# Two-layer hybrid trunk: more projection steps early in the chunk recurrence, and one turn ahead of its Newton step

## The chip, the cores and the metric

One core of a Trainium2 chip. The metric is the device time of one execution in microseconds; the kernel before takes 2350.74 us (median of three runs, 2348.04 to 2352.05). TensorE is called PE here, VectorE DVE, ScalarE ACT, GpSimd POOL, and SyncE, which issues the transfers, SP.

## The reference

Two layers run over 640 tokens of 1024 channels: 128 context tokens and 512 latent ones. Each layer normalises and modulates its input to `h`, projects it (`z = h @ w_in`), and feeds four mixers: a bidirectional recurrent mixer (8 heads with a 64 x 64 state), latent attention, gated position mixing, and a Fourier mixer. Their gated outputs are merged and projected back onto the residual.

The change lies in the recurrent mixer. For each direction it computes, token after token,

```
sa = S @ (-kk)
S  = S * w + outer(sa, kk * a) + outer(v, k)
y  = S @ r
```

for the context (starting from zero) and for the latents (starting from a given state); the outputs of both directions are added.

## The kernel before

All tokens stay on the chip; a tile holds 128 channels in its partitions and the 640 tokens in its columns. A projection chunk of 128 output channels is computed in two halves of 320 tokens. For each of the eight tiles of `h` there are three matmuls (high and low parts of weights and activations), so a half is 24 matmuls; `dense_half` (L161) yields after every two tiles, that is after six matmuls. A chunk is therefore eight such steps, and `fill` (L462), which makes the chunks that later mixers need, adds a ninth when it has stored one to DRAM (`zdr`, L470). Weights come by SP, are rounded by ACT (L144) and the rest is taken by POOL (`wl`, L145).

The recurrence (`recurrence`, L676) goes through 64-token chunks: 2 of the context and 8 of the latents, for two directions, 20 jobs. `intra` (L700) is the part of a job that needs no state. Its steps: loads (L708, L710); decays and keys (L722 to L749); products within the chunk (L757) and their mask; the matrix in two float16 parts; the transposed keys (L776); then the inverse of a 64 x 64 triangular matrix for each head by doubling. The first level starts at L787 to L790; five levels follow, each of two steps: L807 on PE and L808 on DVE, then L814/L815 on PE and the sum L818 on DVE. A Newton step closes it: L823/L824 on PE with L826 on DVE, then L830/L833 with the copy L835 and two copies L838 on ACT. `chain` (L841) is the part with the state, four steps (L847, L854, L860, L868/L870), in the order of the chunks.

A turn of the main loop (L885) advances each chain and each active job by one step; the chains come first, then the oldest job. A job starts every 6 turns (`STAG`), at most 4 are active (`NACT`). With its 21 steps a job in one turn at its last level stands beside one at level 2, one at its matrix parts and one at its loads. `mix` (L97) emits steps of the `fill` chunks after each turn: 1.2 + 0.1 * (5 - running) of them, so 1.6 while one job runs and 1.3 with four (L1230). What is left is emitted after the last turn.

The kernel is written in a framework that records what is emitted and then orders the instructions of each engine ahead of the run, by the order of emission and its own estimate of when operands and buffers are ready. Each engine then runs its list in that order; a late operand holds all that stands behind it. Chunks of `fill` use three PSUM banks (`d`), the recurrence five (`m`). Behind the recurrence comes the first merge (`merge`, L1126): it loads the branch output (`load_o`, L1113: `f<-odr`, ACT, then DVE or POOL), and its first product (`w_merge`, 48 matmuls) needs only `h`.

Of the kernel before, what the change touches and what calls it, by code (L numbers as in the profile page):

```python
# [14 lines left out]
DRAM = bass.MemoryType.DRAM  # L15
# [3 lines left out]
T = 640  # L19
# [6 lines left out]
RATE_R = 1.2  # L26
RATE_R1 = 0.1
RATE_M = (0.25, 0.5, 0.55, 0.5)
NACT = 4
# [27 lines left out]
def trunk(ctx: ExitStack, tc: tile.TileContext, A: dict, O: dict, dbg: dict):  # L57
# [39 lines left out]
    def mix(main, side, rate):  # L97
        """Emit the steps of main, with rate steps of side after each."""
        owed = 0.0
        for n in main:  # L100
            owed += rate(n) if callable(rate) else rate
            while owed >= 1.0:
                next(side, None)
                owed -= 1.0

    def settle(side):
        """Go on to the end of a projection chunk."""
        while next(side, CHUNK_END) != CHUNK_END:
            pass

# [41 lines left out]
    def wload(src, n, leng=None):  # L152
        """Weights in their high and low parts"""
        hi = wp.tile([128, 512], F32R, tag="wh", name="wh", bufs=3)
        lo = wp.tile([128, 512], F32R, tag="wl", name="wl", bufs=3)
        split(hi[:, :n], lo[:, :n], raw_load(src, n), leng)
        return hi, lo
# [3 lines left out]
    def dense_half(w, K, act, use, q, step=2):  # L161
        """use(tokens, psum) with psum[f, tok] = w^T act for the tokens q, three float32r passes."""
# [21 lines left out]
    def rsqrt(out, x, n=T):  # L184
        """out = x ** -0.5: table value, then one Newton step."""
# [6 lines left out]
    def colsum(lhs, rhs, use):  # L192
        """use(cols, psum) for the two halves of lhs^T rhs"""
        for q in HALVES:
            ps = bank1()[:, :320]
            mm(ps, lhs, rhs[:, q], start=True, stop=True)
            use(q, ps)
# [35 lines left out]
    def ada(l, ns, bufs):  # L233
        """Modulation chunks: the tiles of the contraction in four column groups, summed with the turn to feature-major."""
# [30 lines left out]
    def sum_squares(acc, x, k, q, last=None):  # L265
        """acc[:, q] += x^2; the last of the chunks stays apart, for the sum on the tensor engine."""
# [24 lines left out]
    def norm_tile(l, h, xr, k, q):  # L291
        """h[k] at the tokens q from the normalised x, in its high and low parts"""
# [12 lines left out]
    def norm_first(h, X, q):  # L305
        """The first norm, up to its modulation"""
# [19 lines left out]
    def norm_half(l, h, X, q):  # L326
        """RMSNorm and modulation of one half of the tokens"""
# [8 lines left out]
    # ================= one layer =================  # L336
    def layer(l, X, h, w13):
# [17 lines left out]
        def shift(c, z, out):  # L355
            """out = z + (centred_shift(z) - z) * mu for the chunk c of the projection."""
# [7 lines left out]
        def silu2(c, out):  # L364
            """2 * silu of the chunk c of the projection"""
# [17 lines left out]
        def low_rank(kp, src, w):  # L383
            """tanh(0.5 * (bias + up^T src)) for both directions, in the order of their scans, to DRAM."""
# [30 lines left out]
        def unit(xa, c):  # L415
            """the keys' unit vectors"""
# [7 lines left out]
        def proj_rkv(kp, z13):  # L424
            def turn(c, v):
                """the values, token-major"""
# [15 lines left out]
            for nth, c in enumerate((4, 5, 6, 7, 0, 1, 2, 3, 8, 9, 10, 11)):  # L442
                z = kp.tile([128, T], F32, tag="k", name="rkv")
                # within each half and after the chunk: a step of the low-rank products
# [29 lines left out]
        def attention(z13, xa, side):  # L474
            with tc.tile_pool(name=f"at{l}", bufs=1) as ap_, tc.tile_pool(name=f"a2{l}", bufs=2) as a2:
# [16 lines left out]
                # normalised compressed kv and q  # L492
# [32 lines left out]
                # values, token-major  # L525
                def values(vhalf):
                    vv = a2.tile([128, 6, 4, 128], F32R, tag="vv", name="vv", bufs=1)
                    wv_hi, wv_lo = aload(A["w_v"][l, :, 256 * vhalf:256 * vhalf + 256], 256)
                    for tt in range(6):
# [5 lines left out]
                        # high and low parts side by side; the high part in the rows where the head's output goes  # L535
# [64 lines left out]
                def weighted(pn, vv, pr, j, kt, o):  # L600
                    """add the key block kt (0: context rows, 1-5: latent rows) to the outputs of one head"""
# [74 lines left out]
        def recurrence(y):  # L676
            with tc.tile_pool(name=f"rw{l}", bufs=1) as rw:
# [9 lines left out]
                # block-diagonal operands of a pair of heads; what lies outside the blocks stays zero  # L687
# [12 lines left out]
                def intra(seg, i, d, A16, XZ):  # L700
                    """The state-independent part of one 64-token chunk in one direction (8 heads)."""
# [33 lines left out]
                    # modified keys  # L735
# [4 lines left out]
                    # rows of the products: A keys then K keys for even heads, the other way for odd ones;  # L740
                    # the K keys meet the values and stay in the order of the tokens in both directions
# [9 lines left out]
                    # intra-chunk products, masked  # L751
# [11 lines left out]
                    # A^T - I  # L763
# [3 lines left out]
                    # in two parts of float16  # L767
# [15 lines left out]
                    # X = (I - A)^-1 and its transpose by doubling in float16, then one Newton step  # L783
# [8 lines left out]
                    for lev in range(1, 6):  # L792
                        if lev == 2:
                            # token-major values
# [4 lines left out]
                        # the even blocks of columns of X and the odd ones of its transpose change  # L799
# [19 lines left out]
                        yield  # L819
                    ps = bank1()  # L820
# [15 lines left out]
                    # the rows of A make room for the queries of the carried state  # L836
# [47 lines left out]
                nact, since, count = NACT, 99, 0  # L884
                while order or active or chains or jobs:  # L885
# [6 lines left out]
                    # the sequential parts first  # L892
                    if order and len(chains) < 2 and order[0] in done and not any(c[0][0] == order[0][0] and c[0][2] == order[0][2] for c in chains):
# [8 lines left out]
                        chains.append((jb, chain(done.pop(jb), d, state[s_, d])))  # L902
                    running = len(chains) + len(active)
# [13 lines left out]
                    yield running  # L917

# [52 lines left out]
        # ---- Fourier mixing: channels first (only the half that the symmetry leaves), then positions with the odd / even symmetry;  # L971
        # channel k of two groups comes as e - d, channel 128 - k as e + d ----
        def fourier():
            with tc.tile_pool(name=f"fd{l}", bufs=1) as c1, tc.tile_pool(name=f"fe{l}", bufs=2) as c2:
# [10 lines left out]
                # cosine and sine parts of the four groups; the cosine parts of channel 64, each in a column of its own  # L985
# [31 lines left out]
                def pos(stat, tts, o, n):  # L1017
                    """over the positions: the product of the stationary operand's tiles with the table at o"""
# [43 lines left out]
        def rec_out(y):  # L1062
            with tc.tile_pool(name=f"gn{l}", bufs=2) as gp:
# [6 lines left out]
                def sums(x, use):  # L1070
                    """use(cols, psum) with the sums over the channels of each head, in two float32r passes"""
# [12 lines left out]
                for c in range(4):  # L1084
# [4 lines left out]
                    # sum of both directions' modified keys, then the bonus  # L1089
# [56 lines left out]
        # ================= emission =================  # L1146
        fl = fill()
        with ExitStack() as es:
# [3 lines left out]
            # the first four chunks wait for the norm, half by half  # L1152
            with tc.tile_pool(name=f"first{l}", bufs=1, side="right") as fp:
# [14 lines left out]
                if l == 0:  # L1168
                    # in the order in which the inputs come: the products over the first four tiles of h
                    # run before the modulation of the others is there  # L1170
# [57 lines left out]
        with tc.tile_pool(name=f"y{l}", bufs=1, side="right") as yp:  # L1228
            y = yp.tile([128, 4, T], F32, name="y")
            mix(recurrence(y), fl, lambda n: RATE_R + RATE_R1 * (5 - n))  # L1230
# [23 lines left out]
    def in_weights(l):  # L1254
        """the weights of the first chunk that a layer computes"""
        return [wload(A["w_in"][l, 13][:, k * 128:k * 128 + 512], 512) for k in (0, 4)]

    def output(l, mh, ml, w0):
        """x + gate * (merged w_out), half of the tokens after the other; what follows starts on the first half."""
# [73 lines left out]
    # ================= program =================  # L1333
# [20 lines left out]
def _layout(i):  # L1354
# [6 lines left out]
    def ktile(w, m):  # L1361
        """[K, M] -> [128, K/128 * m-chunk]: one m-wide column chunk, k-tiles side by side."""
# [12 lines left out]
    # the order in which the Fourier mixing leaves its channels  # L1375
# [52 lines left out]
    # constants of the shapes alone  # L1428
# [79 lines left out]
```

## Time and profile before

| | us |
|---|---|
| runs: median (lowest, highest) | 2350.74 (2348.04, 2352.05) |
| span of the profiled execution, first to last instruction | 2346.5 |
| PE busy / DVE busy / ACT busy / POOL busy | 2204.5 / 1459.3 / 1099.2 / 890.0 |
| recurrence of layer 0 | about 384 to 729 |
| recurrence of layer 1 | about 1543 to 1886 |

The profiled execution has no time of its own in the page beside its span; the median of the runs is 4.2 us above that span. Busy time is the time in which an engine works on at least one instruction; matmuls overlap, so it isn't the sum of their durations. A wait is put down to the instruction that waited and the one that came last before it. PEclk is the clock granted to PE: 1.00 is 2.4 GHz, and a window that mixes it with 1.2 GHz has a value between 0.5 and 1. `fill` appears as tile `f`, matmuls of L168 to L170 as `dps`.

### The profile page before, as it was taken

What the parts mean: (1) busy time and instruction counts of PE and PEld (TensorE: products, weight loads), DVE (VectorE), ACT (ScalarE), POOL (GpSimd) and SP (SyncE); (2) the same over time, 40 slices, a digit from 0 to 9 for tenths busy, and PEclk for the clock granted to TensorE, in tenths of its full rate; (3) what the DMA queues carried; (4) which work ended last, traced back from release to release, by engine and by line L of the source; (5) the groups of instructions that cost most, each with busy time, mean ns of one, the idle gap of its engine ahead of it and who ended that gap; (6) DMA issues with size and microseconds to landing.
All of it is one profiled execution on the core that took longest, in us unless ns stands there. A gap on an engine that the chain in (4) does not pass through costs nothing. (4 is left out here: it accounts for less than half of the span.)

```text
span 2346.5 us, 49722 instructions
## 1 busy us (share of the span) xinstructions
PE 2204.5 (94%) x19662; PEld 2017.0 (86%) x19662; DVE 1459.3 (62%) x2826; ACT 1099.2 (47%) x2387; POOL 890.0 (38%) x894
## 2 busy tenths in 40 slices
PE   6899998898999999999998999989999999999998
PEld 3788898787889998978998888978888899989997
DVE  4767756888884435642267777578888643367325
ACT  4566755444444333432355667544444343344332
POOL 2322124444443344533453221254444334355452
PEclk8999999999999999999999999999999999999999
DMA  7133336333225425556432333362322254254332
GB/s 260 50 105 92 92 91 195 95 109 98 79 65 169 139 85 173 143 194 240 131 121 71 97 98 98 97 213 84 104 77 76 72 171 151 75 172 144 105 106 101
DMA packets 208009, 283.73 MB, mean 121 GB/s; under 512 B 26912, under 2 KB 119712, under 8 KB 207776
## 3 DMA queue, kind: packets, MB, share of 16 engines
q1 hardware_dynamic: 207776, 280.55, 38.2%
q8 instruction: 155, 2.54, 0.5%
q14 instruction: 78, 0.64, 0.1%
HBM read 224.75 MB, written 55.74 MB: 120 GB/s over the span
## 5 line engine op out<-in xcount | busy, mean ns | idle before, releaser
L145 POOL TENSOR_TENSOR wl<-wr,wh 128x512 fp32r<-128x512 f32 x371 | 520.7, 1407 | 988.4 <-ACT wh L144 846.0
L168 PE MATMUL dps<-hhi,wh 128*128 128x320 f32 x2368 | 773.4, 327 | 12.9 <-DVE f L1133 4.9
L169 PE MATMUL dps<-hlo,wh 128*128 128x320 f32 x2368 | 744.1, 314 | 7.4 <-POOL hlo L299 4.5
L170 PE MATMUL dps<-hhi,wl 128*128 128x320 f32 x2368 | 742.5, 314 | 0.8 <-POOL wl L145 0.8
L168 PEld LDWEIGHTS dps<-hhi,wh 128*128 128x128 f32 x2368 | 452.2, 191 | 33.2 <-issue 8.2
L169 PEld LDWEIGHTS dps<-hlo,wh 128*128 128x128 f32 x2368 | 452.5, 191 | 15.4 <-POOL hlo L299 6.8
L170 PEld LDWEIGHTS dps<-hhi,wl 128*128 128x128 f32 x2368 | 451.5, 191 | 6.1 <-issue 3.7
L144 ACT CAST wh<-wr 128x512 fp32r<-128x512 f32 x372 | 229.3, 619 | 290.4 <-PE dps L169 175.0
L169 PE MATMUL dps<-olo,wh 128*128 128x320 f32 x512 | 161.5, 316 | 9.5 <-POOL olo L145 5.2
L168 PE MATMUL dps<-ohi,wh 128*128 128x320 f32 x512 | 161.2, 316 | 3.7 <-ACT ohi L144 3.6
L170 PE MATMUL dps<-ohi,wl 128*128 128x320 f32 x512 | 159.3, 311 | 0.0
L818 DVE TENSOR_TENSOR XZ<-XZ,m 128x512 f16<-128x512 f16 x200 | 129.5, 677 | 47.9 <-PE m L815 47.7
L1133 DVE SCALAR_TENSOR_TENSOR f<-f,dps 128x320 f32<-128x320 f32 x96 | 46.4, 485 | 138.8 <-PE dps L170 127.1
L765 POOL TENSOR_TENSOR GG<-GG,con 64x256 f32<-64x256 f32 x80 | 61.2, 765 | 163.6 <-DVE GG L760 160.3
L1131 ACT ACTIVATE f<-dps,der 128x320 f32<-128x320 f32 x128 | 67.2, 525 | 113.9 <-PE dps L170 112.1
L169 PEld LDWEIGHTS dps<-olo,wh 128*128 128x128 f32 x512 | 97.1, 190 | 14.8 <-POOL olo L145 6.8
L168 PEld LDWEIGHTS dps<-ohi,wh 128*128 128x128 f32 x512 | 96.8, 189 | 6.9 <-ACT ohi L144 5.0
L170 PEld LDWEIGHTS dps<-ohi,wl 128*128 128x128 f32 x512 | 97.2, 190 | 0.0
L808 DVE TENSOR_TENSOR T<-m,con 128x256 f16<-128x256 f32 x200 | 80.5, 415 | 18.1 <-PE m L807 17.6
L611 DVE TENSOR_TENSOR pl<-m,ph 128x512 fp32r<-128x512 f32 (+1 forms) x96 | 59.3, 620 | 28.5 <-ACT ph L610 27.3
L770 ACT CAST A<-GG 64x256 f16<-64x256 f32 x80 | 32.3, 404 | 90.9 <-POOL GG L765 90.9
L814 PE MATMUL m<-T,XZ 128*128 128x64 f16 x800 | 66.1, 195 | 5.8 <-DVE T L808 5.8
(492 smaller groups left out, 4645.4 us busy)
## 6 DMA issues: line engine op xcount, KB each, us to landing
wr<-in_w_in SPq DMA_DIRECT2D x180, 256.0 KB, 3.0
wr<-in_w_merge SPq DMA_DIRECT2D x128, 256.0 KB, 2.9
ar<-in_w_ada SPq DMA_DIRECT2D x48, 512.0 KB, 6.6
wr<-in_w_branch SPq DMA_DIRECT2D x64, 256.0 KB, 2.8
zdr<-f SPq DMA_DIRECT2D x48, 320.0 KB, 3.5
rk<-spill SPq DMA_DIRECT2D x20, 768.0 KB, 6.0
thdr<-t SPq DMA_DIRECT2D x32, 320.0 KB, 2.9
odr<-t SPq DMA_DIRECT2D x32, 320.0 KB, 3.4
```

What stands on the lines that cost most here:

```text
L144: S_.copy(hi, src)
L145: (leng or G).tensor_sub(lo, src, hi.bitcast(F32))
L168: mm(ps, hi[:, c], ahi(k)[:, q], start=(k == 0), stop=False)
L169: mm(ps, hi[:, c], alo(k)[:, q], start=False, stop=False)
L170: mm(ps, lo[:, c], ahi(k)[:, q], start=False, stop=(k == K - 1))
L611: V.tensor_sub(pl[:, 0:w], tp[:, 0:w], ph[:, 0:w].bitcast(F32))
L765: G.tensor_sub(GK[HALF[j], j], GK[HALF[j], j], bc(i64[HALF[j]], 4))
L808: V.tensor_mul(T1.rearrange("p u (j k o i) -> p (u j) k o i", j=2, o=2, i=b)[:, :, :, 0, :], ps[:, 0:256].rearrange("p (x k i) -> p x k i" ...
L814: mm(ps[:, 64 * u:64 * u + 64], X1[:, u, :], cols(T1[:, u, :], 0), start=True, stop=True)
L818: V.tensor_add(new, new, ps.rearrange("p (x n i) -> p x n i", x=2, i=b))
L1131: yield from dense(A["w_merge"][l, m, n], 8, H, lambda q, ps: S_.activation(gt[:, q], ps, AF.Tanh, scale=0.5, bias=bias))
L1133: yield from dense(A["w_branch"][l, n, m], 4, o, lambda q, ps: V.scalar_tensor_tensor(to[:, q], gt[:, q], 1.0, ps, op0=ALU.add, op1=ALU.mult))
```

## The change

`intra` gets one more `yield`, after the last doubling level and ahead of the Newton step: a job has 22 steps. The rate of `fill` steps is now yielded by the recurrence itself: 3.5 for each of the first 4 turns, 2.0 for turns 5 to 18, and from there the same 1.2 + 0.1 * (5 - running). Comments and docstrings are removed as well.

```diff
                         V.tensor_add(new, new, ps.rearrange("p (x n i) -> p x n i", x=2, i=b))
                         yield
+                    yield
                     ps = bank1()
                     for u, j in units:
...
-                nact, since, count = NACT, 99, 0
+                nact, since, count, turn = NACT, 99, 0, 0
                 while order or active or chains or jobs:
...
                         chains.append((jb, chain(done.pop(jb), d, state[s_, d])))
+
+                    turn += 1
+                    lead = 3.5 if turn <= 4 else 2.0 if turn <= 18 else None
                     running = len(chains) + len(active)
...
-                    yield running
+                    yield lead or RATE_R + RATE_R1 * (5 - running)
...
-            mix(recurrence(y), fl, lambda n: RATE_R + RATE_R1 * (5 - n))
+            mix(recurrence(y), fl, lambda rate: rate)
             run(fl)
```

## Rows read from the trace of the kernel before

**Rows 1.** The page, busy us (share of the span) and instructions of each engine.

```profile
PE 2204.5 (94%) x19662; PEld 2017.0 (86%) x19662; DVE 1459.3 (62%) x2826; ACT 1099.2 (47%) x2387; POOL 890.0 (38%) x894
```

**Rows 2.** Windows: stretch, length, busy PE PEld DVE ACT POOL, clock, DMA share, GB/s.

```profile
384.00:440.00 56.00, 44.84 (x520) 40.64 (x518) 45.52 (x92) 25.83 (x63) 30.93 (x42) 0.94 0.55 181
440.00:728.00 288.00, 273.04 (x4228) 240.38 (x4226) 230.20 (x491) 123.31 (x307) 120.64 (x158) 0.98 0.27 83
...
1543.00:1600.00 57.00, 45.01 (x527) 40.49 (x526) 46.40 (x94) 26.00 (x64) 32.06 (x45) 0.97 0.57 184
1600.00:1886.00 286.00, 270.89 (x4253) 238.50 (x4251) 230.58 (x491) 123.07 (x307) 120.25 (x158) 0.99 0.27 85
```

**Rows 3.** Line L818, who waited for it: us in total, times.

```profile
  PE m L823: 30.8, 28
  PE m L807: 4.0, 18
```

**Rows 4.** Waits of PE, 440 to 728: us in total, times, longest.

```profile
PE m L823 <- DVE XZ L818: 13.4, 12, 1.8
```

**Rows 5.** Waits of PE in the start-up, layer 0, then layer 1.

```profile
PE m L814 <- DVE T L808: 2.4, 4, 1.0
PE m L823 <- DVE XZ L818: 2.0, 2, 1.3
...
PE m L757 <- DMA thl<-thdr: 4.2, 1, 4.2
```

**Rows 6.** Windows of 5 us with a lower clock.

```profile
395.00:400.00 5.00, 3.83 (x22) 3.64 (x23) 3.02 (x8) 1.88 (x5) 3.21 (x4) 0.56 0.60 189
400.00:405.00 5.00, 4.60 (x26) 4.32 (x26) 5.00 (x8) 4.25 (x12) 4.65 (x9) 0.75 0.69 243
455.00:460.00 5.00, 3.69 (x44) 3.31 (x44) 2.49 (x5) 1.95 (x5) 0.51 (x2) 0.71 0.27 79
...
1745.00:1750.00 5.00, 5.00 (x64) 4.38 (x63) 1.72 (x4) 2.74 (x8) 0.57 (x1) 0.77 0.13 47
```

**Rows 7.** Timeline of a turn change: start, us, engine, line, operation, [idle before <- releaser].

```profile
566.36 0.69 PE L870 MATMUL m<-GG,ZZ 128*64 128x64 f32 x16
...
566.98 0.20 PE L814 MATMUL m<-T,XZ 128*128 128x64 f16 x1
...
567.76 1.28 POOL L145 TENSOR_TENSOR wl<-wr,wh 128x512 fp32r<-128x512 f32 x1
567.79 1.40 DVE L843 COPY ZZ<-S 64x256 f32<-64x256 f32 x1
...
569.12 1.27 DVE L818 TENSOR_TENSOR XZ<-XZ,m 128x512 f16<-128x512 f16 x2
...
569.84 0.22 PE L823 MATMUL m<-XZ,A 64*64 64x64 f16 x2 [1.26 <-DVE XZ L818]
```

**Rows 8.** Timeline: two products of a projection, with L169 and L170 between.

```profile
374.83 0.31 PE L168 MATMUL dps<-hhi,wh 128*128 128x320 f32 x1
...
375.27 0.31 PE L168 MATMUL dps<-hhi,wh 128*128 128x320 f32 x1
```

**Rows 9.** Timeline around the first job's products.

```profile
386.01 0.42 ACT L348 COPY f<-dps 128x320 f32<-128x320 f32 x1
...
396.17 1.22 PE L757 MATMUL m<-Qs,Ks 64*128 64x128 f32 x6 [4.45 <-issue]
```

**Rows 10.** Stores of kept projections, layer 0: first and last of 20.

```profile
386.46 0.32 SPq L470 DMA_DIRECT2D zdr<-f  x1
...
726.18 1.65 SPq L470 DMA_DIRECT2D zdr<-f  x1
```

**Rows 11.** Windows over the end of the recurrence, layer 0.

```profile
704.00:729.00 25.00, 25.00 (x383) 21.74 (x383) 10.11 (x22) 6.04 (x14) 5.11 (x4) 1.00 0.27 81
729.00:738.20 9.20, 8.65 (x66) 7.99 (x62) 1.29 (x3) 6.23 (x9) 4.53 (x3) 1.00 0.80 262
```

**Rows 12.** Line L790: ns min/median/max, first and last start.

```profile
L790 DVE TENSOR_TENSOR XZ<-A,m1T x40: 412/559/1156, 403.2 to 1846.6; 128x512 f16<-128x512 f16 x40
```

## The prediction

> **What bounds the kernel now.** I read the page's busy row first: TensorE (PE) is busy 94% of the span, VectorE (DVE) 62% [rows 1]. So time can only come from the 142 us in which PE is idle, or from stretches in which it is busy at the lower clock. The windows over the two recurrences, the only stage the change touches, say where that is [rows 2]: in layer 0 PE is idle 11.2 us of the first 56 and 15.0 us of the next 288; in layer 1 12.0 us of 57 and 15.1 us of 286. Together 53 us.
>
> The waits by line name the causes. After the start-up, 13.4 of the 15.0 us in layer 0 is one wait: L823, the first product of the Newton step, for the sum of the last doubling level, L818 [rows 4]; over both layers 30.8 us in 28 waits [rows 3]. In the start-up the largest single wait is L757 of the first job, 4.5 us in layer 0 [rows 9] and 4.2 in layer 1, where the load of its decays is named; L823 has only 2.0 us there, the rest is several waits of about 1 us, such as L814 for L808 [rows 5].
>
> The timeline of one turn change shows how the L823 wait arises [rows 7]. PE issues 16 products L814/L815 from 566.98, the last ending at 567.6, and then one step of a kept projection; by 568.6 it has nothing left in its order. DVE meanwhile is in the copy L843, which takes 1.40 us beside a POOL subtraction of 1.28 us, and starts the two sums L818 only at 569.12. L823 starts at 569.84, after 1.26 us of waiting. The turns on either side carry more PE work, which is why L818 is late only here.
>
> Last, the clock. Six separate stretches behind these waits (four in layer 0, two in layer 1) show a granted clock down to between 0.66 and 0.77 in a window of 5 us, where the rest shows 1.00; the first and the last are in [rows 6]. Each loses about 1.7 us, the first 0.29*5 = 1.45 in its own window and the rest in the next; the six 10.2 us. Behind the 4.5 us idle at the start of layer 0 the windows show 0.56 and 0.75: 3.4 us.
>
> **The extra turn.** One `yield` delays L823 by a turn; no instruction is added. The 139 turns of layer 0 take 384 to 729, 2.5 us each, and the longest wait is 1.8, so L818 will be ready and the L823 wait should go: **-30.8 us**. What is late next? Before, L823 stood in front of the next younger job's L807, which needs the other half of the same pair of sums; that L807 waited only 4.0 us in all [rows 3] because L823 had waited for it. Now the chain's last step, moved by the same turn, stands there instead, two groups of 16 matmuls of 0.69 us [rows 7]. So that L807 comes 0.88 (one step) + 1.4 = 2.3 us behind L814/L815, where the pair of sums ended (569.12 + 1.27 = 570.39) 2.8 us behind it: up to 0.5 us of wait, nothing where the turn has two steps. Two turns later the youngest doubling job loses about 0.3 us of PE cover, since the chain's 0.69 us group is replaced by the shorter second Newton product. I take 0.2 us for each of 40 jobs, **+8 us**; the ends are 0 and 23 (three quarters of the wait return).
>
> With the waits shorter than those that low-clock stretches followed, I take **-8 us** of the 10.2 (ends 0 and -10.2). A job lives 22 turns instead of 21 and starts every 6, so still four are alive, and A16, XZ (three copies) have a job's first write three turns behind the last read of the job three before. The turn itself costs nothing while other jobs fill PE; at the end of each recurrence it is one turn without any work of its own.
>
> **More kept projections at the start.** A chunk is nine steps, eight with six matmuls. Their pitch is (375.27 - 374.83)/3 = 0.147 us [rows 8], so a step is 0.88 us and a chunk 7.0 us. Layer 0 stores 20 chunks from 386.46 to 726.18 [rows 10]: 180 steps. Before, turns 1 to 18 emit 6*1.6 + 6*1.5 + 6*1.4 = 27 steps; after, 4*3.5 + 14*2.0 = 42. So 15 steps, 13.3 of them with matmuls, 11.7 us of PE work per layer, go from the end to the start. They bring no work and no transfer that wasn't there.
>
> What they meet: by the time PE reached the first L757, it had run the first chunk and, between that chunk's last evacuation at 386.01 and the idle before 396.17, (391.72 - 386.1)/0.147 = 38 of the second's 48 matmuls [rows 9]: 15 steps, where the turns before had emitted 6. The order of an engine is therefore not that of emission while work is missing; 14 emitted steps don't get past those 15, and I leave the 4.5 and 4.2 us where they are (ends: 0, or all 8.7 and 5 us of clock gained). But behind it the turns 5 to 23 got only some 18 steps (27 + 5*1.3 - 15), and now get 33. There the remaining idle of the start-up, 11.2 - 4.5 - 2.0 = 4.7 us in layer 0 and 12.0 - 4.2 - 2.0 = 5.8 in layer 1, has work to cover it. I take two thirds, **-7 us** (ends 0 and -10.5): DVE is busy 5.00 of 5 us at 400 [rows 6], so some turns will be late whatever PE does.
>
> A row and a rule bear on that. The same DVE instruction L790 takes 0.41 us at least and 1.16 at most [rows 12], and L843 1.40 us beside the POOL subtraction [rows 7]. Each chunk brings two such subtractions, so the 1.67 chunks moved put 3.3*1.28 = 4.3 us of POOL beside a full DVE. The Trainium skill, page "SBUF — State Buffer", section "SBUF: two separate sides", says that the two engines share a port pair that the one that starts first holds for its whole instruction, so that the other is blocked fully. By that, all 4.3 us per layer would be added to DVE and the gain of 7 would be gone, which leaves -22.8 and 2328; the rows show such delays, but not beside every subtraction, so I keep 7.
>
> **The price at the end.** All 180 steps are emitted by turn 136 of 139 before, by 128 of 140 after. PE has no idle at all in 704 to 729 of layer 0 and 0.55 us in the 9.2 us behind it [rows 11]. From turn 128 on 11 steps, 9.7 us, are missing. The first gate product of the merge (48 matmuls, 7.0 us) can move up in their place, as ten of its matmuls already did; but today it covers the loading and splitting of the branch output right behind the recurrence. So per layer the loss lies between 0 (the turns shrink by what left them) and 9.7 + 7.0 = 16.7 us. Without the projections the last 12 turns need some 1.2 us each for product, evacuation and the way back, 14.5 us with 10 us of PE's own work; 7.0 us of merge fit in with about 2.5 too much. I take 4 us per layer, **+8 us**.
>
> **Sum:** -30.8 + 8 - 8 - 7 + 8 = -29.8 us. Span 2346.5 - 29.8 = 2316.7; the median of the runs lies 4.2 us above the span, so **2321 us**, 1.3% less.
>
> **Rivals.**
> *The wait only moves.* DVE's order of prepared work and sums stays, and L807 and L814 wait where L823 did. For it: 4.0 us of L807 waits on the same sum. Against it: mid-recurrence DVE is busy 230 of 288 us. Three quarters return: -30.8 + 23 - 5 (clock) - 4 (start) + 8 = -9: 2342.
> *Slower: the bare end.* Place: turns 128 to 140 and the 8 us behind them. Price 16.7 per layer, 33.4, if those turns are bound by their chain today; and the low-clock stretches aren't saved, only moved behind the new idle, as 4.5 us idle brought one at 395. -30.8 + 8 - 7 + 33.4 = +3.6: 2354. It decides once the end costs more than 15 us per layer.
> *The start is fully covered.* The L757 idle goes too with its low clock (-13.7), the end costs 2 per layer (-4): -48, 2303.
> *The rates do nothing.* If order follows readiness alone, the projections run when they do now: no -7, no +8. -31, 2320; only the store times tell it from the forecast.
>
> **Chances.** Forecast 0.46, with an own range of 2310 to 2334; moved wait 0.17; bare end 0.15; covered start 0.12; rates without effect 0.10. A change under 0.2% (4.7 us) can't be told from none. Faster: 0.44 + 0.10 + 0 + 0.12 + 0.09 = 0.75; within 0.2%: 0.01 + 0.06 + 0 + 0 + 0.01 = 0.08; slower 0.01 + 0.01 + 0.15 = 0.17. The range 2302 to 2350 leaves out the bare end and little else.
>
> **What would show it.** L823's waits for L818 at under 3 us in all, and none of L807 above 12. No window below 0.9 of the clock between 440 and 690. The third and fourth stores of layer 0 behind 386 some 8 us earlier in relation to L757 of job 4, the last store before the last L870. L757's first wait still 4 us. PE idle in the last 25 us of the recurrence and the 9 behind, 3 to 6 us, where it was 0.6. It is wrong if the waits of PE in mid-recurrence add up to over 10 us per layer, or the end to over 10.

## The result: 0.6% slower, and the profile after

The changed kernel takes 2367.6 us (median of four runs, 2363.06 to 2369.59) where the kernel before, timed beside it, takes 2351.39 (2348.04 to 2352.36): a ratio of 1.0062, interval 1.0045 to 1.0078. Forecast were 2321 us and a range of 2302 to 2350; it is slower, and outside the range. The profiled execution took 2369.59 us, its span is 2367.8, so 21.3 us more than the span of before. In the code after, lines behind the added `yield` have numbers higher by one: the Newton step is L824/L825, the chain's steps L848, L855, L861 and L869/L871, the two copies between its second and third step L856 (DVE) and L857 (ACT).

The page's busy row, against [rows 1]:

```profile
PE 2217.0 (94%) x19662; PEld 2022.8 (85%) x19662; DVE 1475.3 (62%) x2826; ACT 1102.1 (47%) x2387; POOL 886.7 (37%) x894
```

Windows like [rows 2] (stretch, length, busy PE PEld DVE ACT POOL, clock, DMA share, GB/s): the two recurrences, then the end of layer 0's recurrence and the first microseconds behind it, as in [rows 11].

```profile
384.00:440.00 56.00, 46.35 (x460) 43.10 (x459) 38.99 (x73) 22.49 (x55) 30.39 (x36) 0.94 0.60 200
440.00:734.00 294.00, 275.69 (x4309) 237.93 (x4308) 243.61 (x507) 126.07 (x313) 119.18 (x163) 0.99 0.25 80
...
1556.00:1613.00 57.00, 48.70 (x473) 45.45 (x472) 39.95 (x77) 23.77 (x57) 30.80 (x39) 0.94 0.65 208
1613.00:1907.00 294.00, 275.67 (x4299) 238.01 (x4297) 243.72 (x507) 126.09 (x313) 119.19 (x163) 0.99 0.26 80
710.00:735.00 25.00, 25.00 (x436) 21.21 (x434) 13.59 (x31) 5.31 (x15) 2.55 (x2) 1.00 0.17 49
735.00:744.20 9.20, 6.50 (x35) 5.33 (x36) 2.43 (x3) 7.80 (x11) 6.16 (x4) 0.89 0.81 251
740.00:750.00 10.00, 8.62 (x39) 7.78 (x39) 3.21 (x6) 6.33 (x12) 2.36 (x3) 0.66 0.99 344
```

In the first 56 us PE idles 9.7 us instead of 11.2, in layer 1 8.3 of 57 instead of 12.0, though the same stretch now holds less of the recurrence (460 matmuls instead of 520, 473 instead of 527). In mid-recurrence PE idles 18.3 us in each layer, where it was 15.0 and 15.1, although the wait that made up nearly all of it has gone. The waits of PE from 440 to 734 (us in total, times, longest), against [rows 4], and who waited for L818 in the whole span, against [rows 3], tell why.

```profile
PE m L861 <- ACT ZZ L857: 10.0, 12, 1.5
PE m L861 <- DVE ZZ L856: 4.0, 6, 1.3
PE m L807 <- DVE XZ L818: 2.8, 3, 2.2
PE m L814 <- DVE T L808: 0.9, 1, 0.9
```

```profile
  PE m L807: 5.6, 6
```

The Newton step waits for nothing any more; 30.8 us are gone. In their place stands L861, the third step of the chain, with 14.0 us in layer 0 and the same 14.0 in layer 1; before, this step had no wait. It waits for the copies of the chain's second step, 20.1 of the 28.0 us for the one on ACT. One such place, in the timeline (start, us, engine, line, operation, [idle before <- releaser]):

```profile
571.98 0.68 PE L855 MATMUL m<-R,Z 64*64 64x64 f32 x16
572.59 0.41 PE L807 MATMUL m<-XZ,A 128*128 128x64 f16 x8
...
573.92 0.33 PE L861 MATMUL m<-ZZ,KT 128*64 128x64 f32 x2
575.75 0.68 PE L861 MATMUL m<-ZZ,KT 128*64 128x64 f32 x14 [1.50 <-ACT ZZ L857]
...
572.52 1.61 POOL L765 TENSOR_TENSOR GG<-GG,con 64x256 f32<-64x256 f32 x2 [1.96 <-DVE GG L760]
...
573.28 0.41 ACT L770 CAST A<-GG 64x256 f16<-64x256 f32 x1 [0.60 <-POOL GG L765]
574.16 0.40 ACT L770 CAST A<-GG 64x256 f16<-64x256 f32 x1 [0.47 <-POOL GG L765]
574.90 0.41 ACT L839 COPY GG<-Qs 64x256 f32<-64x256 f32 x1 [0.34 <-POOL Alo L772]
575.33 0.37 ACT L857 COPY ZZ<-m 64x256 f32<-64x256 f32 x1
```

L855 ends at 572.66, but its ACT copy L857 starts at 575.33: ahead of it in ACT's list stand the two casts L770 of a younger job and a copy L839 of the same job, and all three wait for POOL's subtractions L765 and L772 (0.60, 0.47 and 0.34 us). In the kernel before, this ACT copy started 0.5 to 0.9 us behind the chain's second product; now it is 1.6 to 2.9 us behind it in 17 of layer 0's 20 jobs, and in 16 of the 20 the instruction just ahead of it is L770 or L839. PE meanwhile has 8 small products and one projection step (572.84 to 573.95).

The idle time understates such a wait. The end of a matmul is modelled, so the first part of a wait counts as busy: the first two products of L861 start at 573.92 and the next at 575.75, and of these 1.83 us only 1.50 are called idle. So the stretches are also counted from the start of one matmul to the start of the next, and put down to the later of the two; the text says "from start to start" where it does that.

From the timelines I took the start of the third chain and of the eighteenth; between them lie 15 periods of six turns. "Projection matmuls" are those of L168 to L170. By these marks the stages are (us, layer 0 / layer 1):

| stage | before | after | difference |
|---|---|---|---|
| start, to the third chain (from 384 and 1543.0; after, from the same matmuls at 382.7 and 1556.4) | 77.6 / 76.7 | 88.2 / 89.3 | +10.6 / +12.6 |
| middle, 15 periods | 235.8 / 234.5 | 240.3 / 239.1 | +4.5 / +4.6 |
| from there to the last product of the recurrence | 31.9 / 32.0 | 23.7 / 23.6 | -8.2 / -8.4 |

So the start takes most of what was moved into it (90 and 89 projection matmuls, 13 us at 0.147), the end is shorter by what left it (57 in each layer, 8.4 us), and the middle, where the gain should have been, is longer:

```profile
470.90:711.20 240.30, 225.62 (x3487) 194.72 (x3486) 205.12 (x428) 107.06 (x266) 102.92 (x141) 0.99 0.27 87
```

Against the kernel before (its line stands under the first experiments, with those of e3 and e2) PE is idle 2.0 us more there and busy 2.5 more, with 14 matmuls fewer. From start to start, layer 0's middle has 16.3 us more at L861 (26.8 for 10.5; idle shows 11.3 of it) and 3.9 more at L807, against 12.5 less at the Newton step's first products; projection matmuls, 12 fewer, take 2.4 less and the rest 0.8 less. That is the 4.5 us. In layer 1 it is +16.3, +3.5, -12.8, -2.1 and -0.4. More has come back than went.

The stages make 15.7 us. The other 5.6 of the spans lie outside, nearly all between the recurrences (1120 to 1555 in the profile before): that code, which no edit touches, took 436.0 us before, 441.6 after and 437.7 to 441.8 in the other sixteen traces, so the difference can't be put down to these edits. The medians are 16.2 apart, not 21.3.

### The profile page after: what moved, and what is told of

Its sections match the earlier page's. It is cut to its first block, busy times and chain, and to the rows that moved or that the text cites. A ratio compares the mean times of both kernels' runs of the same rounds, so it can differ in the third digit from the quotient of the medians.

```text
span 2367.8 us, 49714 instructions
## 1 busy us (share of the span) xinstructions
PE 2217.0 (94%) x19662; PEld 2022.8 (85%) x19662; DVE 1475.3 (62%) x2826; ACT 1102.1 (47%) x2387; POOL 886.7 (37%) x894
## 5 line engine op out<-in xcount | busy, mean ns | idle before, releaser
L168 PE MATMUL dps<-hhi,wh 128*128 128x320 f32 x2368 | 771.6, 326 | 17.6 <-ACT f L1135 8.1
L169 PE MATMUL dps<-hlo,wh 128*128 128x320 f32 x2368 | 743.0, 314 | 7.6 <-POOL hlo L299 3.9
L170 PE MATMUL dps<-hhi,wl 128*128 128x320 f32 x2368 | 743.6, 314 | 0.0
L168 PEld LDWEIGHTS dps<-hhi,wh 128*128 128x128 f32 x2368 | 451.0, 190 | 39.2 <-ACT f L1135 9.1
L169 PEld LDWEIGHTS dps<-hlo,wh 128*128 128x128 f32 x2368 | 451.4, 191 | 16.4 <-POOL hlo L299 6.6
L170 PEld LDWEIGHTS dps<-hhi,wl 128*128 128x128 f32 x2368 | 450.7, 190 | 5.0 <-issue 3.7
L169 PE MATMUL dps<-olo,wh 128*128 128x320 f32 x512 | 163.2, 319 | 9.4 <-POOL olo L145 4.8
L168 PE MATMUL dps<-ohi,wh 128*128 128x320 f32 x512 | 163.8, 320 | 3.9 <-ACT ohi L144 3.9
L170 PE MATMUL dps<-ohi,wl 128*128 128x320 f32 x512 | 161.0, 314 | 0.0
L818 DVE TENSOR_TENSOR XZ<-XZ,m 128x512 f16<-128x512 f16 x200 | 132.5, 681 | 39.6 <-PE m L815 39.5
L765 POOL TENSOR_TENSOR GG<-GG,con 64x256 f32<-64x256 f32 x80 | 60.5, 757 | 144.3 <-DVE GG L760 141.3
L169 PEld LDWEIGHTS dps<-olo,wh 128*128 128x128 f32 x512 | 98.7, 193 | 14.5 <-DVE olo L145 6.7
L168 PEld LDWEIGHTS dps<-ohi,wh 128*128 128x128 f32 x512 | 98.4, 192 | 7.2 <-ACT ohi L144 5.4
L170 PEld LDWEIGHTS dps<-ohi,wl 128*128 128x128 f32 x512 | 98.8, 193 | 0.0
L808 DVE TENSOR_TENSOR T<-m,con 128x256 f16<-128x256 f32 x200 | 78.8, 415 | 16.7 <-PE m L807 14.9
L814 PE MATMUL m<-T,XZ 128*128 128x64 f16 x800 | 65.9, 194 | 4.6 <-DVE T L808 4.6
L594 ACT ACTIVATE pe<-sps,st 128x640 f32<-128x640 f32 x64 | 50.8, 794 | 40.3 <-DVE st L592 40.2
```

Of the source, the lines that this page charges most:

```text
L168: mm(ps, hi[:, c], ahi(k)[:, q], start=(k == 0), stop=False)
L169: mm(ps, hi[:, c], alo(k)[:, q], start=False, stop=False)
L170: mm(ps, lo[:, c], ahi(k)[:, q], start=False, stop=(k == K - 1))
L594: S_.activation(pe[:, 0:kn].rearrange("p (b n) -> p b n", n=hn), sv, AF.Exp, bias=st[:, 1:2], scale=scale, accum_out=st[:, 2:3])
L765: G.tensor_sub(GK[HALF[j], j], GK[HALF[j], j], bc(i64[HALF[j]], 4))
L808: V.tensor_mul(T1.rearrange("p u (j k o i) -> p (u j) k o i", j=2, o=2, i=b)[:, :, :, 0, :], ps[:, 0:256].rearrange("p (x k i) -> p x k i" ...
```

## The experiments

Sixteen kernels, each timed in three rounds. The kernel before took 2351.91 us beside e1 to e4 (16 runs), 2351.9 beside e5 to e8 (19), 2351.24 beside e9 to e12 (25) and 2349.93 beside e13 to e16 (8). Ratios are against the runs beside them and have their 95% interval in brackets. Turns are counted from 1. "Cover" is the projection work that PE has between two steps of the recurrence, "the lead" the start's higher rates, and "alignment" which turns the projection steps fall into.

### Each edit alone, and projection steps put where PE waits

**e1**, the extra turn alone (the first hunk of the diff). **e2**, the start's rates alone (the others). **e3**, the kernel before, and **e4**, the extra turn, both with as many projection steps in the middle as before, but more of them in the one turn after which PE waits:

```diff
+                    turn += 1
                     running = len(chains) + len(active)
+                    rate = RATE_R + RATE_R1 * (5 - running)
+                    if 18 < turn <= 121:
+                        rate = 2.0 if turn % 6 == 1 else 1.14   # e4: turn % 6 == 0
...
-                    yield running
+                    yield rate
```

Expected of e1:

> The extra turn alone, the rates of fill steps as before. Theory A (the rates cost, by the end of the recurrence left bare; the turn only moves the wait from L823 to the chain's third step): 2351 us within 5, PE waits of 12 to 16 us per layer at the third chain step (L861), none at the Newton step, and the last store of a kept projection still within 2 us of the last chain's end. Theory B (the turn costs, because the chain now stands in the turns with the least cover and the periods of six turns grow from 15.8 to 16.1 us): 2360 to 2370, with the period of mid-recurrence at 16.1 or more.

Expected of e2:

> The higher rates in turns 1 to 18 alone, a job has 21 steps as before. Theory A (the rates cost): 2362 to 2370; the L823 waits stay at 30 us, the start-up is 7 to 10 us longer per layer, the end only 6 to 9 shorter, and the first merge after layer 0 starts some 5 to 8 us poorer with a window of low clock. Theory B (the turn costs): 2345 to 2353.

Expected of e3:

> The kernel before, with the same number of fill steps in each six turns of mid-recurrence (7.7), but two of them in the turn whose end is the L823 wait and 1.14 in each of the others. Theory C (the wait is a matter of how little PE work stands between the last sum and its reader): the L823 waits of turns 20 to 121 fall from 13 us per layer to under 4, none of the others grows over 4, and the time falls by 12 to 25 us, to 2325 to 2340. Theory D (DVE with its prepared work is the limit, a wait that is taken away returns at another reader): the PE waits in mid-recurrence stay over 10 us per layer and the time within 5 us of 2351.

Expected of e4:

> The extra turn, rates at the start as before, and in mid-recurrence two fill steps in the turn that ends in the chain's third step (L861), 1.14 in each of the others. Theory C: the L861 waits fall from about 14 us per layer to under 4 and the time lies 12 to 25 us under that of the extra turn alone. Theory D: the waits stay over 10 us per layer at other lines and the time within 5 us of the extra turn alone.

| | us | ratio |
|---|---|---|
| e1 extra turn alone | 2363.46 | 1.0046 [1.0033, 1.0060] |
| e2 start's rates alone | 2379.28 | 1.0114 [1.0091, 1.0137] |
| e3 before, cover at the Newton step | 2330.93 | 0.9909 [0.9893, 0.9926] |
| e4 extra turn, cover at the third step | 2349.12 | 0.9987 [0.9977, 0.9996] |

Each edit alone is slower; the extra turn costs 12 us, the rates 27, and together they cost 16, not 39. e3 beats the kernel before by 21 us and leaves every step of a job in its turn. Waits of PE over the recurrence of layer 0 (384 to 735), in the kernel before, e1, e3 and e4:

```profile
PE m L823 <- DVE XZ L818: 15.4, 14, 1.8
```

```profile
PE m L861 <- ACT ZZ L857: 13.3, 16, 1.5
...
PE m L861 <- DVE ZZ L856: 2.4, 3, 1.9
```

```profile
PE m L823 <- DVE XZ L818: 7.6, 8, 1.7
```

```profile
PE m L807 <- DVE XZ L818: 7.4, 10, 2.2
PE m L861 <- ACT ZZ L857: 6.5, 13, 0.9
...
PE m L861 <- DVE ZZ L856: 1.1, 2, 0.9
```

The windows over the 15 middle periods, of the kernel before, e3 and e2:

```profile
461.60:697.40 235.80, 223.16 (x3501) 196.70 (x3500) 198.04 (x424) 106.21 (x266) 105.19 (x141) 0.98 0.28 86
```

```profile
457.00:684.20 227.20, 219.28 (x3499) 193.26 (x3498) 198.22 (x423) 106.22 (x266) 105.20 (x142) 1.00 0.29 90
```

```profile
467.40:715.10 247.70, 229.59 (x3499) 202.39 (x3498) 203.85 (x430) 106.62 (x267) 104.31 (x142) 0.95 0.27 85
```

All three run 3500 matmuls there, within two. Against the kernel before, e3 idles 4.7 us less (7.9 for 12.6) and is busy 3.9 us less with the same matmuls, at a clock of 1.00 instead of 0.98: that is its 8.6 us. e2 idles 5.5 us more and is busy 6.4 more, at a clock of 0.95. One place of e2 shows how the two hang together:

```profile
560.35 0.31 PE L170 MATMUL dps<-hhi,wl 128*128 128x320 f32 x1
562.89 0.22 PE L823 MATMUL m<-XZ,A 64*64 64x64 f16 x2 [2.23 <-DVE XZ L818]
...
564.97 0.47 PE L168 MATMUL dps<-hhi,wh 128*128 128x320 f32 x1
565.24 0.47 PE L169 MATMUL dps<-hlo,wh 128*128 128x320 f32 x1
```

A wait of 2.23 us, and two microseconds behind its end the projection's matmuls go at a pitch of 0.27 us instead of 0.147 [rows 8].

The cover can be counted: in the timelines I counted the projection matmuls that PE runs between the last product of the step before and the one that waits, for each of layer 0's 20 jobs (a step is 6 matmuls).

| wait of | projection matmuls in between | jobs | wait, us |
|---|---|---|---|
| L823, before | 4 to 7 / 12 | 18 / 2 | 15.4 / 0 |
| L823, e3 | 4 to 7 / 12 | 6 / 14 | 6.5 / 1.1 |
| L861, after | 2 to 7 / 12 | 15 / 5 | 12.6 / 1.4 |
| L861, e1 | 2 to 7 / 12 | 15 / 5 | 13.7 / 2.0 |

With about one step a job waits 0.8 to 1.1 us in the mean, with two 0 to 0.4. So theory C stands in its mechanism: the wait hangs on how many steps fall into that turn. Its figure for the waits does not: it had said under 4 us, and 7.6 are left at L823 in e3 and at L861 in e4. By the code, five of e3's six jobs with about one step got a chunk's ninth step, which has no matmul, as one of their two. Theory D (DVE as the limit) falls with e3's time, though in e4 a wait does return at another reader, 7.4 us at L807. Theory A is refuted by e1, theory B by e2, which is 9 us above A's range as well. e4 is 14 us under e1, at the lower end of its 12 to 25.

### Why the extra turn costs: the longer job or the chain's place

```diff
 # e5: the kernel before, the extra turn at the job's start
                     thw, tha = th[:, 0:4, :], th[:, 4:8, :]
                     yield
+                    yield
...
 # e9: the kernel before, an empty turn at the chain's start; e10: e1 with the same
                     Qs, ZZ, GK, GR, Z1, KT, PC, ch, first = it
+                    yield
```

Expected of e5:

> The kernel before, with the one extra turn at the other end of the chunk job: after the job's loads, ahead of its first computation. The job has 22 steps as in the changed kernel, but its later steps keep their places against the chain of carried states and against the neighbouring jobs. Theory P (what costs in the changed kernel is the chain's new place against the neighbouring jobs): the waits behind the ZZ copies at the chain's third step do not come, those at the inverse's Newton step stay near 15 us in a layer, and the time is that of before, 2349 to 2356. Theory N (a job of one more step is dearer wherever the step is, since five runs instead of four stand in more turns and each such turn gets fewer projection steps): 2360 to 2366, as the kernel with the extra turn alone.

Expected of e9:

> The kernel before, with an empty turn at the start of the chain of carried states instead of ahead of the Newton step: the job keeps its 21 steps and its own places, the four steps of the chain stand one turn later against the jobs, as they do in the changed kernel. Theory P (the chain's new place brings the new waits): 8 to 16 us in a layer appear ahead of the chain's third step, behind the ZZ copies; the chain's fourth step now stands ahead of the Newton step in its turn and takes a part of the wait there (15 us before, under 10 now). Both together about even or dearer: 2350 to 2366. Theory N (the longer job costs, not the place): no waits of over 4 us in a layer at the third step and 2346 to 2355.

Expected of e10:

> The kernel with the extra turn alone (e1), and an empty turn at the start of the chain besides: the chain's second and third step then have a turn between them in which two jobs run the second halves of a doubling level (16 matmuls each), not one in which jobs have first halves of 4 each. Theory P: the waits at the third step fall from 16 us in a layer to under 6, those at the Newton step stay away, and the time is 8 to 18 us under e1, 2345 to 2356. Theory N: the job is as long as in e1 and the chain longer, so 2362 to 2370.

e5 took 2358.0 us (1.0021 [1.0011, 1.0031]), e9 2355.89 (1.0024 [1.0014, 1.0033]), e10 2358.88 (1.0031 [1.0016, 1.0045]). Waits of PE over layer 0's recurrence, in e5, e9 and e10 (in e5 the Newton step is L824 and the second half of a level L815; in e10 the chain's second and third steps are L856 and L862):

```profile
PE m L824 <- DVE XZ L819: 12.1, 12, 1.5
PE m L815 <- DVE T L809: 8.9, 13, 1.9
```

```profile
PE m L861 <- ACT ZZ L857: 11.9, 15, 1.5
...
PE m L861 <- DVE ZZ L856: 3.7, 4, 1.9
...
PE m L823 <- DVE XZ L818: 0.8, 1, 0.8
```

```profile
PE m L862 <- ACT ZZ L858: 6.1, 7, 1.4
...
PE m L856 <- ACT R L851: 3.0, 4, 0.9
...
PE m L862 <- DVE ZZ L857: 1.3, 4, 0.4
```

e9 is the cleanest. The job is as long as before and the Newton step where it was; only the chain is a turn later (and the projection steps are dealt to the turns as in e1, since the longer chain counts as running). The waits at the third step come, 15.6 us as in e1 (15.7), and those at L823 go, 15.4 to 0.8, because the chain's fourth step (32 matmuls) now stands just ahead of it, in 19 of layer 0's 20 jobs. So the new place of the chain is what makes the new wait, and it is enough to remove the old one. e5, with the longer job and the chain in its old place, has no wait at the third step and still 12.1 us at the Newton step, nearly what theory P said; but 8.9 us of waits have come ahead of the second half of a level (2.6 before), and its time is 2 us over P's range and 2 under N's. In e10 the third step's waits halve (7.4) but do not fall under 6 as P said; the middle is 8.3 us shorter than e1's, the start 6.0 longer with one more turn for the chain, and 4.6 us of time are left, not 8 to 18: the time is outside both theories' ranges. Against the kernel before, the chain's place alone costs 4.7 us (e9), the longer job alone 6.1 (e5), and the extra turn, which does both, 11.6 (e1).

### Why the start's rates cost 27 us

```diff
 # e6: e3 with the start's rates
+                    if turn <= 18:
+                        rate = 3.5 if turn <= 4 else 2.0
...
 # e7: the kernel before, half a step more in the first turn; e13: half a step less
+                    if turn == 1:
+                        rate += 0.5
 # e14, e15: e2 with half a step less, half a step more; e16: both edits, half a step less
```

Expected of e6:

> The kernel before with the changed kernel's projection rates in turns 1 to 18 and, in turns 19 to 121, the rates of e3 (2.0 in the turn that holds the Newton step's wait, 1.14 in the others). Theory M (the 27 us that the lead rates cost alone are lost in the middle of the recurrence, where the projection steps are as many as before but fall worse, so that idle time grows and the clock drops): a middle made by the phase rule gives most of it back, idle and clock loss there as in e3, and what stays is the start, the bare end and the joins, some 4 to 5 us in a layer: 2337 to 2345. Theory S (the lead costs by itself, through the transfers and buffers that it pulls forward): 2352 to 2360, 27 us over e3.

Expected of e7:

> The kernel before with half a projection step more credited in the first turn alone: every projection step of the recurrence then comes up to one turn earlier or at the same turn, and nothing else is changed. Theory M: the middle's time hangs on which turn a projection step falls into, so even this moves the time by more than 0.2 per cent, by 5 to 15 us to either side. Theory S: nothing of note moves, 2349 to 2355.

Expected of e13:

> The kernel before with half a projection step less credited in the first turn, the counterpart of e7. Theory A (the middle's time hangs on which step falls into which turn, and the kernel before has a good one of several alignments): it moves by 2 to 10 us, more likely up. Theory R (what a half step does is within 3 us, and e7's 4.6 is nearly all there is): 2349 to 2354.

Expected of e14:

> The start's rates alone (e2) with half a projection step less in the first turn. Theory A (a large part of e2's 27 us is its alignment: one step of projection, at times the empty last one of a chunk, ahead of the Newton step): it comes down by 5 to 15 us, 2363 to 2374. Theory R (the lead costs 27 us whatever the alignment): 2376 to 2383.

Expected of e15:

> The start's rates alone (e2) with half a projection step more in the first turn. As for the half step less: theory A 2360 to 2374, theory R 2376 to 2383. If the two half steps fall on both sides of 2379, e2 is an ordinary alignment and its cost is the lead's.

Expected of e16:

> The changed kernel, both edits, with half a projection step less in the first turn. Theory A: another alignment, 3 to 8 us off 2367 to either side. Theory R: 2364 to 2370.

Times in us, with the half step credited in the first turn:

| | half a step less | as it was | half a step more |
|---|---|---|---|
| kernel before | 2366.0 (e13) | 2349.9 to 2351.9 | 2356.66 (e7) |
| start's rates alone | 2361.84 (e14) | 2379.28 (e2) | 2357.42 (e15) |
| both edits | 2367.96 (e16) | 2367.6 | not tried |

Half a step, 0.44 us of PE work, moves the kernel before by +16 (e13's ratio is 1.0066 [1.0051, 1.0081]) or +5 us (e7's is 1.0019 [1.0009, 1.0030], just outside both of its ranges), and e2 by -17 or -22. e13, e14 and e15 moved further than theory A had said, to the sides that it had named. The reason is in the waits, in e13 and then in e15:

```profile
PE m L823 <- DVE XZ L818: 11.6, 12, 2.2
PE m L814 <- DVE T L808: 10.1, 12, 1.9
```

```profile
PE m L823 <- DVE XZ L818: 14.6, 13, 1.9
...
PE m L814 <- DVE T L808: 1.6, 2, 1.4
```

Some 7.7 projection steps fall into six turns, and a chunk is nine steps, one of which has no matmul. Which turn gets the second step is settled by the fraction that the first turns leave behind, and which turn gets the empty one by the number of steps dealt before. In e13, as in e2 (L823 13.9, L814 6.4), the shortage also falls ahead of L814 within a doubling level, from start to start 9.9 and 6.6 us more than before; in e15, as in the kernel before, hardly.

e2 deals 15 whole steps more than the kernel before, so by the code its second steps fall into the same turns from turn 19 to 125, and only the empty ones move. e7, e13, e14 and e15 share one other dealing of second steps. There the lead costs -4 us (e14 against e13) and +1 (e15 against e7), where e2 loses 27. e6, in which the rule of e3 fixes the middle, took 2338.12 us (0.9940 [0.9924, 0.9955]): 7 over e3, inside theory M's range. So most of e2's 27 us is its alignment, and the lead's own cost is between -4 and +7 us in these pairs. That e16 does not differ from the changed kernel, as theory R said, shows that not every half step matters.

### Better versions, and the changed kernel with cover

e8 and e11 are e3 with other shares; e12 has both edits and e4's rule.

```diff
+                        rate = 2.6 if turn % 6 == 1 else 1.02                # e8
...
+                        rate = {1: 2.3, 2: 1.4}.get(turn % 6, 1.0)           # e11
```

Expected of e8:

> e3 with the same number of projection steps in six turns, but 2.6 in the turn of the Newton step's wait and 1.02 in the others. If the cover at this turn is what sets the wait, the waits that e3 has left there (0.5 to 1.7 us, eight of them in a layer) shrink to nearly nothing and the time is 2322 to 2329. If the other turns are then too thin (the rows of the changed kernel show waits of 0.3 to 1.5 us in turns with one step), it is 2331 to 2342.

Expected of e11:

> e3 with 7.7 projection steps in six turns as before, spread as 2.3 in the turn ahead of the Newton step's first products, 1.4 in the next (ahead of its second products, where the 2.6 of e8 left waits of up to 2.4 us for Dm) and 1.0 in the four others. Theory C (cover at the turns whose wait is longest sets the middle): idle in the middle 5 to 7 us in a layer instead of 7.9, 2324 to 2330. If the thinner four turns cost as much as the two gain, it stays at 2330 to 2335.

Expected of e12:

> The changed kernel with both of its edits, and in turns 19 to 121 the rates of e4 (2.0 in the turn ahead of the chain's third step, 1.14 in the others). Theory M (the start's rates cost some 7 us over the two layers by the bare end and the joins, as from e3 to e6, and the rest of the loss is in the middle, where it is a matter of cover): e4 and 4 to 9 us, 2353 to 2358, and 10 to 14 under the changed kernel. Theory S (the lead costs in the middle whatever the cover there): 2362 to 2370.

e8 took 2330.68 us (0.9907 [0.9892, 0.9922]), e11 2328.95 (0.9909 [0.9888, 0.9930]): both as e3, within the error; e8 lies between its two ranges. In e8 the waits left at L823 fall from 7.6 to 3.2 us in layer 0, but the next turn, now thin, brings 5.6 at L833; e11 has 4.9 and 3.2, and its idle in layer 0's middle is 8.3 us, not the 5 to 7 that theory C gave. Neither gains on e3. e12 took 2354.53 us (1.0013 [1.0004, 1.0023]), 5 over e4 and 13 under the changed kernel, as theory M said.

## Why the prediction was wrong, step by step

**What bounds the kernel: right, and read too narrowly.** The wait at L823 was there and is gone with the turn, all 30.8 us of it. But what sets the middle is which step stands behind too little PE work, and that is not tied to L823.

**"What is late next?" is the step that failed.** The prediction followed what stood behind the Newton step and found L807 (5.6 us now, 4.0 before, so it was right there), and put 8 us, at most 23, on what comes back. It named the chain's last step only as new cover. But the chain starts when its job ends, so all of its steps moved a turn against the other jobs, and its second and third step came to stand on both sides of a turn with 8 small products and little else, with the copy between them behind a younger job's ACT work. That brought 28.0 us back at L861, and 1.6 at L807: 29.6 for the 8 that the sum had. e9 makes the wait at L861 without the extra turn. The rival "the wait only moves" was right that the wait returns at another reader, but it had 23 us, L807 and L814 as the place, and DVE's order as the cause; it is ACT's copy that 20.1 of the 28.0 us wait for. By the prediction's own sign (over 10 us of waits in mid-recurrence) it was wrong: they are 17.7 us in each layer.

**The clock: -8 forecast.** Two windows of 5 us between 440 and 690 are still under 0.9, and three in layer 1; their losses add up to 6.7 us (3.3 and 3.4) instead of 10.2: -3.5. The term rested on the waits getting shorter. Those at L861 are, up to 1.5 us, but one of 2.2 us at L807 in each layer is longer than any before (1.8), and layer 0's one stretch at the lower clock lies beside it.

**The start: -7 forecast.** Up to the third chain, before and after, layer 0 and then layer 1:

```profile
384.00:461.60 77.60, 64.13 (x791) 57.51 (x789) 63.54 (x126) 34.96 (x86) 39.98 (x53) 0.93 0.45 147
382.70:470.90 88.20, 74.92 (x887) 68.22 (x885) 66.83 (x128) 37.76 (x93) 44.11 (x57) 0.96 0.44 144
...
1543.00:1619.70 76.70, 62.40 (x796) 55.63 (x794) 63.94 (x126) 34.89 (x86) 40.13 (x56) 0.98 0.46 150
1556.40:1645.70 89.30, 77.39 (x893) 70.42 (x891) 66.97 (x129) 37.88 (x93) 44.39 (x59) 0.94 0.45 145
```

PE's idle fell from 13.5 to 13.3 us and from 14.3 to 11.9, -2.6 in all; so this term was too large by 4. The windows of [rows 2] would give -5.2, but they hold less of the recurrence after. The wait at L757 stayed (5.3 and 4.3 us) as said. The Trainium skill's page "SBUF — State Buffer", section "SBUF: two separate sides", would have let DVE's lock-out take this gain. DVE is busy 3.3 and 3.0 us longer here, with 2 and 3 instructions more and 4.1 and 4.3 us more of POOL beside it, part of which may be that; but in the middle it is busy 7.1 us longer with less POOL work (102.92 us for 105.19), and no run isolates it.

**The bare end: +8 forecast.** PE has no idle in the last 25 us, but 2.7 us in the 9.2 behind, where it was 0.55, at a clock of 0.89; the 10 us from 740 to 750 are at 0.66, 3.4 us lost. That is 2.2 + 3.4 = 5.6 us in this layer; in layer 1 it is 1.5 + 1.7 = 3.2. Together 8.8, near the forecast. e6 over e3, start and end together, is +7 where the prediction has -7 + 8 = +1, which also says that the start's gain was put too high. Of the rivals on the rates none came true: the wait at L757 stayed, each end cost less than 15 us, and 89 or 90 projection matmuls more did run in each start.

**What the sum had no term for.** Both edits change which turn gets which projection step: the extra turn through the rate, which falls when more jobs run, the lead through the place of the empty ninth steps. The prediction treated the steps of the middle as fixed cover; half a step more or less is worth 0 to 22 us here, as much as most of its terms. Put together, the terms as idle and clock show them are -30.8 + 29.6 - 3.5 - 2.6 + 8.8 = +1.5, and the span is 21.3 longer: 5.6 of the rest lie outside the recurrences, and from start to start the new waits less the old ones are 14.7 us in the two middles, where idle shows 4.0. How much of the time is alignment no run tells. The evidence was in the trace of before: of 20 jobs of layer 0, 18 had about one step ahead of L823, and 14 of them waited; two had two steps and didn't.

**What stays open.** With the cover set in both, the extra turn costs 18 us (e4 over e3). From start to start, the 9.9 us of layer 0's middle are 10.2 more at L861 and 6.6 more at L807, 6.1 less at the Newton step and 0.8 less in the rest; so it is the new waits, though idle time shows only 4.3 of it. No run changed the order of ACT's list, so that the copy L857, moved ahead of the younger job's work, would take the wait away is not shown. Nor can e5's 6 us for a longer job be told from what a new alignment may cost: its 8.9 us ahead of the second half of a level look like e13's 10.1.

## What to carry to other kernels

When a step of a pipelined loop is moved by a turn, list every step that starts because of it, and for each the work in the turn ahead of it and what its copies stand behind on the other engines; here the wait came back at the pair with too little in between. Where filler work is dealt out by a fractional rate, put the second portion into the turn that waits (here -21 us) rather than removing the turn's wait by structure. And time a change that does nothing, such as half a filler step, before a few tenths of a per cent are put down to a cause.

## What the runs showed that was not expected

Some of the longest waits cost time a second time, through the clock. In e2 the wait of 2.23 us that ends at 562.89 is followed by a stretch from 563.8 to 567.1 at half the clock (pitch 0.27 instead of 0.147 us), which costs about 1.7 us more. Others are not followed by one: 1.93 us at L814 in e13, 1.90 us at L861 in e16. In e3's middle no stretch at the lower clock is left: of its 8.6 us, 4.7 came from idle time and 3.9 from time that counts as busy, of which the projection matmuls, as many as before, have 2.1.

The kernel is deterministic enough for its alignment to show: the periods of six turns in e2 are 18.2, 17.9, 16.6, 20.0, 15.5 and 14.8 us in layer 0 (from the fifth on), and 18.3, 18.2, 16.7, 20.0, 15.5 and 14.8 in layer 1.
